# A delta-rule recurrence on one core: nine-block operands, sums moved into the matmul accumulator, four chain banks, and copies moved from VectorE to ScalarE

## The chip, the core and the metric

The kernel runs on one core of a Trainium2 chip. A core has a matrix engine (TensorE: PE for its matmuls, PEld for the loads of its stationary operand), VectorE (DVE), ScalarE (ACT), GpSimd (POOL), and SyncE (SP), which here only issues transfers. All engines work through queues of their own in order and wait for each other by semaphores. Matmuls write to PSUM, eight banks of 128 partitions by 512 f32 values. The metric is the device time of one execution in microseconds (us); lower is better.

## What is computed

The reference is a trunk of four layers: a gated spatial unit, an RWKV-7 layer, a latent attention layer, and a second gated unit. All is f32. The change lies in the RWKV layer alone. Its heart is a recurrence over 256 context tokens and 256 tokens that start from the context's state, for 16 heads of width 64, in two directions; the directions' outputs are added and normalized per head:

```python
def step(S, inp):
    w_t, k_t, v_t, kk_t, a_t = inp[:5]
    s_kk = jnp.einsum('nbhvk,nbhk->nbhv', S, kk_t)
    S = S * w_t[..., None, :] - s_kk[..., :, None] * (kk_t * a_t)[..., None, :] + v_t[..., :, None] * k_t[..., None, :]
    y_t = jnp.einsum('nbhvk,nbhk->nbhv', S, inp[5]) if emit else None
    return S, y_t
...
y = ys[0] + jnp.flip(ys[1], axis=1)
...
mean = jnp.mean(yh, axis=-1, keepdims=True)
var = jnp.mean(jnp.square(yh - mean), axis=-1, keepdims=True)
yn = ((yh - mean) * lax.rsqrt(var + RWKV_LN_EPS)).reshape(y.shape) * ln_gain + ln_bias
```

## The kernel before, in words

The recurrence is done in chunks of 64 tokens: eight chunks (four of the context, four of the sequence), one after the other. The 16 heads are split into four groups g of four heads; with the two directions a group has four "lanes" l (direction n, pair pr), and each lane holds two heads h, one in partitions 0 to 63 and one in 64 to 127 (`H[h]`).

Per group there are these pieces of work:

- `features` makes the operands of four lanes, one lane after another: on GpSimd a `+1` (L659) and the products K (L694), on VectorE a running sum (L667), the products AR (L680, L681), a few more (L685, L688) and the products B (L695). K and B go to the tile BK, eight tiles per group, in the form `[128, 4 chunks, 2, 64]`. For head h, block h of a chunk holds K and block 1-h holds B, so that a chunk's two blocks are one matmul operand of 128 columns.
- `inverse` solves a 64 by 64 triangular system per chunk and head: matmuls `nab` (L717), copies, a transpose, a loop of 31 steps of two VectorE operations each (L734, L735), transposes back (L739, L741) and small matmuls `pg` (L754) and `px` (L765).
- `operands`, per pair of chunks: matmuls `pe` (L785) into the two PSUM banks of tag "s", masked by VectorE into E (L789), loads of UV, and four 128 by 128 transposes of BK per chunk (`pbk`, L805) into the one bank of tag "t", copied by ScalarE to BKT (L806).
- `chain`, per chunk: `pz` (L829, L831), copied by ScalarE to Z (L833); `pu` (L838), whose halves are copied into UV, one by ScalarE (L839) and one by VectorE (L840); `py` from the old state (L845); `pd` (L852), to which VectorE adds the old state (L856) and multiplies by the decay (L857), which gives the new state S; and `py` from UV (L861). `py` holds both directions. The first direction that reaches a place of Y is copied there by ScalarE (L870), and the second is added by VectorE (L872).
- `gate` (matmuls `pg`, L895), `bonus`, `normed` and `added` (matmuls `op`, L966) turn Y into the layer's output. `normed` takes the mean over each head by a matmul with the block matrix `bdm` (`pmean`, L937), subtracts it on VectorE (L938), squares on ScalarE (L941), takes the variance by another matmul (`pvar`, L943) and multiplies (L945).

Tag "c" has three PSUM banks. pz, pu, py, pd, pg, the bonus, the mean, the variance and op of the first three groups all take them in turn. Tags "f" and "n" have one bank each.

`interleave` merges the source of these pieces: while the chain of group g runs, the features and the inverse of group g+1, the gates of g and the output of earlier groups are laid around it. The framework that builds the program then orders each engine's instructions further by their dependencies, so the order on an engine is not strictly that of the source. Values and the features and inverse of group 0 come before the first chain.

## Time before, and the profile

| what | us |
|---|---|
| median of three runs | 1627.66 (1627.23 to 1628.16) |
| the profiled execution | 1626.01 |
| its span, first to last instruction | 1623.8 |
| PE busy | 1521.5 |
| DVE busy | 1173.6 |
| ACT busy | 786.9 |
| POOL busy | 123.3 |

Times in the views are counted from the start of the span. The RWKV recurrence, from the values to the last output, lies between 548 and about 1057 us. An f32 matmul appears as two matmul records (two passes), each with its own weight load; a transpose appears as one. A matmul's record includes the time in which its result runs out of the array, so a record of a back-to-back matmul is longer than its place in the queue: what one costs is read from start to start. The granted clock (PEclk) is the share of TensorE's full 2.4 GHz that it was given; 0.5 is 1.2 GHz.

### The profile page before, as it was taken

Reading aid. Unit: us, or ns where it says so; the run is one execution under the profiler, and the core shown is the slowest. Engines: PE = TensorE matmul, PEld = TensorE weight load, DVE = VectorE, ACT = ScalarE, POOL = GpSimd, SP = SyncE. Lnnn points to the kernel's source line nnn. Section 1 sums busy time; section 2 is a strip of 40 time slices with the busy share of each in tenths; the row PEclk is TensorE's granted clock in tenths of the full one; section 3 lists DMA queues with packets and bytes.
Section 4 is the critical chain, followed back from the end, with each engine's and each line's share of the span. In section 5 each row is a group of like instructions: output and inputs, shape, how many; then the busy total and the mean of one; then the engine's idle time right before and its main releaser. Section 6 shows DMA issues by size and latency. Waiting matters only on the chain.

```text
span 1623.8 us, 28689 instructions
## 1 busy us (share of the span) xinstructions
PE 1521.5 (94%) x11538; PEld 1182.9 (73%) x11538; DVE 1173.6 (72%) x2133; ACT 786.9 (48%) x1404; POOL 123.3 (8%) x156
## 2 busy tenths in 40 slices
PE   5999999999599998999999999889999999979999
PEld 2787888888466644776776777778777777768887
DVE  3789998844878376687877964778765666665876
ACT  4534321232456343435345333469876766456543
POOL 0000000000600232302203100000000000000000
PEclk9999999999799998899999999989999999989999
DMA  9675668531144552522322132144321232265552
GB/s 363 252 281 226 233 212 306 208 104 52 52 143 169 161 164 66 157 92 76 118 91 85 61 106 88 67 144 136 118 83 43 73 99 91 66 233 186 177 182 78
DMA packets 95173, 229.03 MB, mean 141 GB/s; under 512 B 26048, under 2 KB 52160, under 8 KB 80576
## 3 DMA queue, kind: packets, MB, share of 16 engines
q1 hardware_dynamic: 92736, 223.00, 40.6%
q10 hardware_dynamic: 2304, 4.20, 0.7%
q8 instruction: 91, 1.49, 0.4%
q14 instruction: 42, 0.34, 0.1%
HBM read 208.81 MB, written 17.83 MB: 140 GB/s over the span
## 4 chain that ended last, share of the span: by engine, by line
PE 49%; DVE 14%; ACT 3%; issue 2%; POOL 1%; DMA 1%; ACTq 0%; DVEq 0%
PE fm L310 5%; PE op L310 4%; PE op L966 2%; PE fm L311 2%; PE pg L895 2%; DVE Tm L735 2%; DVE tmp L734 2%; PE op L311 2%; PE pu L310 2%; PE pz L310 2%; PE po L1277 2%; PE sc L1295 2%; PE pe L785 2%; PE sc L1296 1%; DVE BK L695 1%
## 5 line engine op out<-in xcount | busy, mean ns | idle before, releaser
L184 DVE TENSOR_TENSOR lo<-raw,hi 128x2048 fp32r<-128x2048 f32 (+3 forms) x147 | 247.1, 1682 | 105.2 <-ACT hi L183 104.5
L183 ACT CAST hi<-raw 128x2048 fp32r<-128x2048 f32 (+3 forms) x161 | 212.3, 1324 | 217.5 <-PE op L314 40.5
L251 DVE SCALAR_TENSOR_TENSOR junk<-adaw,scb 128x1024 f32<-128x1024 f32 x112 | 136.8, 1222 | 8.7 <-DMA adaw<-in_ada_wT 6.7
L310 PE MATMUL op<-s,hi 128*128 128x512 f32 x256 | 91.5, 400 | 0.0
L375 PE MATMUL pv<-hi,hp 128*128 128x512 f32 x192 | 76.4, 400 | 9.1 <-ACT hi L183 6.0
L376 PE MATMUL pv<-lo,hp 128*128 128x512 f32 x192 | 76.2, 397 | 1.7 <-DVE lo L184 1.7
L310 PE MATMUL fm<-hx,hi 128*128 128x512 f32 x200 | 73.8, 409 | 4.1 <-ACT hx L304 3.8
L377 PE MATMUL pv<-hi,hp 128*128 128x512 f32 x192 | 75.9, 395 | 0.0
L311 PE MATMUL op<-s,lo 128*128 128x256 f32 x256 | 71.3, 281 | 0.0
L895 PE MATMUL pg<-xz,wz 128*128 128x256 f32 x256 | 68.7, 408 | 0.0
L313 PE MATMUL pj<-xs,hi 128*128 128x512 f32 x128 | 53.6, 420 | 12.5 <-ACT xs L304 10.2
L311 PE MATMUL fm<-hx,lo 128*128 128x256 f32 x200 | 56.6, 288 | 2.0 <-DVE lo L184 2.0
L995 PE MATMUL pv<-wv,xv 128*128 128x512 f32 x128 | 57.3, 596 | 0.0
L310 PEld LDWEIGHTS op<-s,hi 128*128 128x128 f32 x256 | 48.0, 188 | 12.4 <-issue 1.3
L314 PE MATMUL pj<-xs,hi 128*128 128x512 f32 x128 | 52.2, 408 | 5.0 <-DVE xs L305 5.0
L694 POOL TENSOR_TENSOR BK<-f 64x256 f32<-64x256 f32 x64 | 53.5, 836 | 38.1 <-DVE f L688 30.7
L785 PE MATMUL pe<-AR,BK 64*128 64x128 f32 x512 | 53.8, 306 | 2.2 <-DVE E L789 2.0
L310 PE MATMUL fm<-cq,hi 128*128 128x512 f32 x144 | 55.7, 423 | 0.0
L895 PEld LDWEIGHTS pg<-xz,wz 128*128 128x128 f32 x256 | 47.8, 198 | 10.0 <-issue 2.1
L315 PE MATMUL pj<-xs,lo 128*128 128x512 f32 x128 | 52.1, 408 | 2.2 <-DVE lo L184 2.1
L313 PE MATMUL pu<-hp,hi 128*128 128x512 f32 x128 | 50.7, 396 | 0.0
L789 DVE TENSOR_TENSOR E<-pe,masks 128x512 f32<-128x512 f32 x64 | 41.9, 683 | 12.1 <-PE pe L785 7.2
(392 smaller groups left out, 4063.2 us busy)
## 6 DMA issues: line engine op xcount, KB each, us to landing
adaw<-in_ada_wT SPq DMA_DIRECT2D x36, 1024.0 KB, 6.2
raw<-in_sgu_v SPq DMA_DIRECT2D x16, 1024.0 KB, 5.5
raw<-in_sgu_u SPq DMA_DIRECT2D x16, 1024.0 KB, 4.9
raw<-in_sgu_z SPq DMA_DIRECT2D x16, 1024.0 KB, 4.8
raw<-in_sgu_o SPq DMA_DIRECT2D x16, 1024.0 KB, 4.8
adaw<-in_ada_w SPq DMA_DIRECT2D x24, 512.0 KB, 10.0
xz<-xz SPq DMA_DIRECT2D x32, 256.0 KB, 3.0
raw<-in_ml_z SPq DMA_DIRECT2D x16, 512.0 KB, 3.7
```

What stands on the lines that cost most here:

```text
L183: S.copy(hi[:, sl], raw[:, sl])
L184: (nc.gpsimd if parts > 1 and i else V).tensor_tensor(lo[:, sl], raw[:, sl], hi[:, sl], ALU.subtract)
L251: V.scalar_tensor_tensor(out=junk, in0=raw[:, f, :], scalar=1.0, in1=scb[:, c, :], op0=ALU.mult, op1=ALU.mult, accum_out=m[:, t * 2 + f, c ...
L310: PE.matmul(p, whi, x, start=start, stop=False)
L311: PE.matmul(p[:, 0:256], wlo, x[:, 0], start=False, stop=stop)
L313: PE.matmul(p, whi, x[:, 0], start=start, stop=False)
L375: PE.matmul(pv[tb], hs[k][:, 0, sl], whi[:, ws_], start=k == 0, stop=False)
L376: PE.matmul(pv[tb], hs[k][:, 0, sl], wlo[:, ws_], start=False, stop=False)
L377: PE.matmul(pv[tb], hs[k][:, 1, sl], whi[:, ws_], start=False, stop=k == 7)
L785: PE.matmul(pe[h][:, j * 128:j * 128 + 128], bk[H[h], i % 4, :, :], ar[H[h], i % 4, :, :], start=True, stop=True)
L895: PE.matmul(p, ws[k // 4][:, k % 4, pr * 128:pr * 128 + 128], xs[k // 2][:, k % 2, :], start=k == 0, stop=k == 7)
L995: PE.matmul(p, xv[:, k, tb * 128:tb * 128 + 128], ws[k // 4][:, k % 4, :], start=k == 0, stop=k == 7)
```

## The change

BK becomes `[128, 9 blocks, 64]` per tile. K of head 0 goes to blocks 0, 2, 4, 6, K of head 1 to blocks 2, 4, 6, 8, and B of both heads to blocks 1, 3, 5, 7, so that one VectorE operation over 128 partitions writes B where there were two over 64. A chunk's operand for head h is two neighbouring blocks from block `2*(i % 4) + h`.

The transposes of BK are done per head: 64 partitions by 128 columns, so eight per chunk where there were four. They go into the two banks of tag "s", one bank for each head, both chunks of a pair side by side, and are copied by ScalarE when both chunks are there. Tag "t" is given up, and tag "c" has four banks.

In the chain the second half of `pu` is copied by ScalarE too. `pd` starts with two matmuls of the identity with the old state, 256 columns each, and accumulates onto them; the VectorE addition is gone. The two directions of `py` are copied to two tiles (Y and Yr), all by ScalarE. `normed` multiplies both by `center` (the identity minus `bdm`) into one accumulator, which is the sum of directions less its mean, so the subtraction is gone; the square and the product read the accumulator.

The scratch memory for GpSimd-generated transfers is set to 1024 bytes, which leaves room for the larger tiles.

```diff
+        center = const.tile([128, 128], F32, name="center")
+        V.tensor_tensor(center, ident, bdm, ALU.subtract)
...
-        env["ps"] = (("f", 1), ("n", 1), ("s", 2), ("t", 1), ("c", 3))
+        env["ps"] = (("f", 1), ("n", 1), ("s", 2), ("c", 4))
...
-                        bk = st(f"BK{sg}", [128, 4, 2, 64], 8)
+                        bk = st(f"BK{sg}", [128, 9, 64], 8)
                         for h in range(2):
-                            nc.gpsimd.tensor_tensor(bk[H[h], :, h, :], k4[H[h], sg], c4[H[h], sg], ALU.mult)
-                            V.scalar_tensor_tensor(out=bk[H[h], :, 1 - h, :], in0=b4[H[h], sg], scalar=-0.5, in1=c4[H[h], sg],
-                                                   op0=ALU.mult, op1=ALU.mult)
+                            nc.gpsimd.tensor_tensor(bk[H[h], 2 * h:2 * h + 7:2, :], k4[H[h], sg], c4[H[h], sg], ALU.mult)
+                        V.scalar_tensor_tensor(out=bk[:, 1:8:2, :], in0=b4[:, sg], scalar=-0.5, in1=c4[:, sg], op0=ALU.mult, op1=ALU.mult)
...
+        def stacked(bk, h, i):
+            j = 2 * (i % 4) + h
+            return bk[H[h], j:j + 2, :].rearrange("p a s -> p (a s)")
...
+            pb = [ps("pbk", "s") for h in range(2)]
             for ii in range(2):
-                bt = d["bk", ii] = ct("BKT", [128, 4, 2, 64], 2)
                 i = i2 * 2 + ii
-                pb = ps("pbk", "t")
                 for l in range(4):
-                    PE.transpose(pb[:, l * 128:l * 128 + 128], f["BK"][l, i // 4][:, i % 4, :, :].rearrange("p a b -> p (a b)"), ident)
-                S.copy(bt.rearrange("p l h k -> p (l h k)"), pb)
-                yield
+                    for h in range(2):
+                        PE.transpose(pb[h][:, (ii * 4 + l) * 64:(ii * 4 + l) * 64 + 64], stacked(f["BK"][l, i // 4], h, i), ident[H[h], H[h]])
+                if ii == 0:
+                    yield
+            for h in range(2):
+                d["bk", h] = ct("BKT", [128, 2, 4, 64], 4)
+                S.copy(d["bk", h].rearrange("p i l k -> p (i l k)"), pb[h])
+            yield
...
-                V.tensor_copy(uv[H[0], 1, ii], pu[H[0]])
+                S.copy(uv[H[0], 1, ii], pu[H[0]])
...
-                    pd = q4(ps("pd", "c"))
+                    pd = ps("pd", "c")[:, 0:256]
+                    if s0 is not None:
+                        for h in range(2):
+                            PE.matmul(pd[H[h]], ident[:, H[h]], s0.rearrange("p l v -> p (l v)"), start=True, stop=False, skip_group_check=True)
+                    pd = pd.rearrange("p (l v) -> p l v", l=4)
                     for l, h in LH:
-                        PE.matmul(pd[H[h], l], bk[:, l, h, :], uv[:, h, ii, l], start=True, stop=True)
+                        PE.matmul(pd[H[h], l], bk[h][:, l, :], uv[:, h, ii, l], start=s0 is None and l == 0, stop=l == 3, skip_group_check=True)
                     sn = ct("S", [128, 4, 64], 2)
-                    pcb = f["12"][:, :, i:i + 1].to_broadcast([128, 4, 64])
-                    if s0 is not None:
-                        V.tensor_tensor(sn, pd, s0, ALU.add)
-                        V.tensor_tensor(sn, sn, pcb, ALU.mult)
-                    else:
-                        V.tensor_tensor(sn, pd, pcb, ALU.mult)
+                    V.tensor_tensor(sn, pd, f["12"][:, :, i:i + 1].to_broadcast([128, 4, 64]), ALU.mult)
...
-                for n in range(2):
-                    y = yt[:, :, (3 - c) * 64:(4 - c) * 64][:, :, ::-1] if n else yt[:, :, c * 64:c * 64 + 64]
-                    if c < 2:
-                        S.copy(y, py[:, n * 2:n * 2 + 2])
-                    else:
-                        V.tensor_tensor(y, y, py[:, n * 2:n * 2 + 2], ALU.add)
+                S.copy(yt[0][:, :, c * 64:c * 64 + 64], py[:, 0:2])
+                S.copy(yt[1][:, :, (3 - c) * 64:(4 - c) * 64][:, :, ::-1], py[:, 2:4])
...
-            PE.matmul(pm, bdm, y, start=True, stop=True)
-            V.tensor_tensor(y, y, pm, ALU.subtract)
+            PE.matmul(pm, center, y, start=True, stop=False)
+            PE.matmul(pm, center, cut(f["Y"][c][1]), start=False, stop=True)
             yield
             sq = cut(ct("fin", [128, 2, 256], 3))
-            S.activation(sq, y, AF.Square)
+            S.activation(sq, pm, AF.Square)
             pq = flat(ps("pvar", next(tags)))
             PE.matmul(pq, bdm, sq, start=True, stop=True)
             state["act"] = rsqrt_bc(sq, pq, 1.0, epsln)
-            V.tensor_tensor(y, y, sq, ALU.mult)
+            V.tensor_tensor(y, pm, sq, ALU.mult)
...
-                f["Y"].append(ct("Y", [128, 2, 256], 3))
+                f["Y"].append([ct("Y", [128, 2, 256], 3), ct("Yr", [128, 2, 256], 3)])
...
-    nc = _bacc.Bacc("TRN2", target_bir_lowering=False, num_devices=1)
+    nc = _bacc.Bacc("TRN2", target_bir_lowering=False, num_devices=1, dynamic_dma_scratch_size=1024)
```

Tag "t" in the lists of banks at the end of the layer becomes "c"; the operand of `nab` (L717) is addressed by its block.

## Rows read from the trace of the kernel before

**Rows 1.** The page's first part: busy time of each engine, its share of the span and its instructions.

```profile
PE 1521.5 (94%) x11538; PEld 1182.9 (73%) x11538; DVE 1173.6 (72%) x2133; ACT 786.9 (48%) x1404; POOL 123.3 (8%) x156
```

**Rows 2.** Ten stretches that cover the recurrence: the stretch, its length in us, the busy us and (instructions) of PE, PEld, DVE, ACT and POOL in this order, the granted clock as a share of 2.4 GHz, the transfers' share and GB/s; the last line adds them up. 548 to 664 is the values with group 0's features and inverse; 664 to 700, 760 to 802 and 867 to 911 hold the features of groups 1, 2 and 3; 700 to 760, 802 to 867 and 911 to 970 their inverses; 970 to 1030 the chain of group 3; 1030 to 1057 the last output.

```profile
548.00:630.00 82.00, 79.37 (x448) 36.82 (x446) 62.01 (x131) 37.39 (x69) 24.28 (x27) 1.00 0.49 132
630.00:664.00 34.00, 27.70 (x387) 22.12 (x387) 19.07 (x31) 14.24 (x24) 10.39 (x13) 0.60 0.43 125
664.00:700.00 36.00, 31.73 (x629) 25.68 (x629) 22.59 (x48) 17.36 (x42) 11.34 (x12) 0.95 0.46 141
700.00:760.00 60.00, 57.84 (x924) 44.31 (x920) 51.34 (x126) 25.68 (x50) 7.85 (x10) 1.00 0.27 81
760.00:802.00 42.00, 37.52 (x574) 27.48 (x573) 34.72 (x68) 22.04 (x45) 15.64 (x18) 0.92 0.35 107
802.00:867.00 65.00, 61.38 (x970) 47.79 (x968) 53.18 (x129) 26.03 (x52) 6.62 (x8) 1.00 0.27 88
867.00:911.00 44.00, 39.23 (x583) 28.75 (x584) 35.43 (x67) 22.21 (x45) 17.54 (x21) 0.92 0.29 86
911.00:970.00 59.00, 55.31 (x896) 43.65 (x895) 45.28 (x116) 20.56 (x40) 2.03 (x4) 1.00 0.28 87
970.00:1030.00 60.00, 58.20 (x828) 45.63 (x828) 27.01 (x59) 21.31 (x46) 0.00 (x0) 1.00 0.32 107
1030.00:1057.00 27.00, 22.47 (x193) 17.95 (x189) 21.88 (x65) 13.96 (x36) 0.00 (x0) 0.95 0.07 22
sum 509.00, PE 470.75 PEld 340.19 DVE 372.51 ACT 220.78 POOL 95.70; mean PE 47.08 PEld 34.02 DVE 37.25 ACT 22.08 POOL 9.57
```

**Rows 3.** Who waited for whom between 548 and 1057 us: the waiting engine and line, the instruction waited for, us in total, times, the longest.

```profile
DVE UV L840 <- ACT UV L839: 22.0, 10, 5.8
PE pg L754 <- DVE Dm L739: 8.4, 4, 5.7
PE pd L852 <- DVE UV L840: 6.8, 6, 2.2
PE pz L829 <- DVE z L900: 3.7, 1, 3.7
PE pe L785 <- DVE E L789: 2.0, 4, 0.7
```

**Rows 4.** The timeline of one chunk of group 1's chain: start, duration, engine, line and operation.

```profile
787.22 0.37 ACT L839 COPY UV<-pu 64x256 f32<-64x256 f32 x1
787.80 1.23 DVE L667 TENSOR_TENSOR_SCAN f<-cmask,f 128x512 f32<-128x512 bf16 x1 [0.68 <-POOL BK L694]
792.25 0.41 DVE L840 COPY UV<-pu 64x256 f32<-64x256 f32 x1
793.33 0.69 PE L852 MATMUL pd<-UV,BKT 128*64 128x64 f32 x16
```

**Rows 5.** Groups of instructions of one line and shape between 548 and 1057 us: count, busy us, mean ns of one, idle time before them.

```profile
L695 DVE SCALAR_TENSOR_TENSOR BK<-f 64x256 f32<-64x256 f32 x64 | 39.5, 617 | 1.5 <-ACT f L670 0.5
L840 DVE COPY UV<-pu 64x256 f32<-64x256 f32 x32 | 13.1, 410 | 22.0 <-ACT UV L839 22.0
L856 DVE TENSOR_TENSOR S<-pd,S 128x256 f32<-128x256 f32 x24 | 10.0, 418 | 4.9 <-PE pd L852 4.8
L872 DVE TENSOR_TENSOR Y<-Y,py 128x128 f32<-128x128 f32 x32 | 8.5, 282 | 0.0
L938 DVE TENSOR_TENSOR Y<-Y,pmean 128x512 f32<-128x512 f32 x7 | 4.8, 684 | 4.0 <-PE pmean L937 4.0
L839 ACT COPY UV<-pu 64x256 f32<-64x256 f32 x32 | 11.7, 367 | 32.9 <-PE pu L838 29.3 <-DMA xz<-xz 3.2
L870 ACT COPY Y<-py 128x128 f32<-128x128 f32 x32 | 7.0, 271 | 11.0 <-PE py L861 11.0
```

**Rows 6.** Line L695 alone: count, least, median and greatest duration in ns.

```profile
L695 DVE SCALAR_TENSOR_TENSOR BK<-f x64: 405/460/972, 562.1 to 903.5; 64x256 f32<-64x256 f32 x64
```

**Rows 7.** TensorE's timeline in a stretch without waits, with the shape of the tile (rows*columns) and of the streamed operand; xN is the number of passes. From the start of a row to the start of the next is what its passes cost.

```profile
970.87 1.16 PE L785 MATMUL pe<-AR,BK 64*128 64x128 f32 x16
971.96 1.99 PE L895 MATMUL pg<-xz,wz 128*128 128x256 f32 x8
973.89 0.69 PE L852 MATMUL pd<-UV,BKT 128*64 128x64 f32 x16
974.40 0.64 PE L861 MATMUL py<-E,UV 128*64 128x64 f32 x16
974.97 1.12 PE L937 MATMUL pmean<-Y,bdm 128*128 128x512 f32 x2
975.93 0.60 PE L805 MATMUL pbk<-ident,BK 128*128 128x128 f32 x4
976.37 1.89 PE L895 MATMUL pg<-xz,wz 128*128 128x256 f32 x8
978.19 0.34 PE L829 MATMUL pz<-UV,E 64*64 64x64 f32 x4
```

**Rows 8.** TensorE's timeline around its longest wait of the recurrence.

```profile
629.53 0.48 PE L643 MATMUL pw<-wx,w2w 128*128 128x512 f32 x1
635.75 1.92 PE L754 MATMUL pg<-Dm,X 32*32 32x32 f32 x64 [5.74 <-DVE Dm L739]
```

More of the change, by code (lines that the diff above doesn't have):

```diff
@@ L717, in inverse @@
                             PE.matmul(pn[64 * h + 32 * hf:64 * h + 32 * hf + 32, i * 64:i * 64 + 64 - 32 * hf],
-                                      bk[H[h], i % 4, 1 - h, 32 * hf:32 * hf + 32], ar[H[h], i % 4, 0, 32 * hf:64], start=True, stop=True)
+                                      bk[H[h], 2 * (i % 4) + 1, 32 * hf:32 * hf + 32], ar[H[h], i % 4, 0, 32 * hf:64], start=True, stop=True)
                 p8 = pn.rearrange("p (i t) -> p i t", i=8)
@@ L784, in operands @@
                             bk, ar = f["BK"][l, i // 4], f["AR"][l, i // 4]
-                            PE.matmul(pe[h][:, j * 128:j * 128 + 128], bk[H[h], i % 4, :, :], ar[H[h], i % 4, :, :], start=True, stop=True)
+                            PE.matmul(pe[h][:, j * 128:j * 128 + 128], stacked(bk, h, i), ar[H[h], i % 4, :, :], start=True, stop=True)
                 for h in range(2):
@@ L824, in chain @@
                 e = lambda l, h: d["E", l % 2, h][:, ii, l // 2]
-                uv, bk = d["uv"], d["bk", ii]
+                uv, bk = d["uv"], [d["bk", h][:, ii] for h in range(2)]
                 q4 = lambda p: p[:, 0:256].rearrange("p (l v) -> p l v", l=4)
@@ L934, in normed @@
             tags = iter("fn" if g == 3 else "cc")
-            y, z, b = cut(f["Y"][c]), cut(f["z"][c]), cut(b)
+            y, z, b = cut(f["Y"][c][0]), cut(f["z"][c]), cut(b)
             pm = flat(ps("pmean", next(tags)))
-            PE.matmul(pm, bdm, y, start=True, stop=True)
-            V.tensor_tensor(y, y, pm, ALU.subtract)
+            PE.matmul(pm, center, y, start=True, stop=False)
+            PE.matmul(pm, center, cut(f["Y"][c][1]), start=False, stop=True)
             yield
             sq = cut(ct("fin", [128, 2, 256], 3))
-            S.activation(sq, y, AF.Square)
+            S.activation(sq, pm, AF.Square)
             pq = flat(ps("pvar", next(tags)))
@@ L959, in added @@
             cut, flat = quarters(q)
-            y = cut(f["Y"][c])
+            y = cut(f["Y"][c][0])
             for oo in range(4):
@@ L1050, in rwkv @@
         ws = [wout(3, oo, t.rearrange("p a (b c) -> p a b c", b=2)) for oo, t in enumerate((wz[0][:, 2:4], wz[1][:, 0:2], wz[1][:, 2:4], ct("z", [128, 2, 256], 3)))]
-        op30 = added(3, f, 0, "csct", ws=ws)
+        op30 = added(3, f, 0, "cscc", ws=ws)
         interleave((islice(steps, 12), 12), (chained(late, normed(3, f, 0), bonus(3, 1, b)), 11))
         interleave((steps, 4), (normed(3, f, 1, b, slice(1, 3)), 4), (islice(op30, 1), 2))
-        interleave((normed(3, f, 1, b, slice(0, 4, 3)), 3), (chained(op30, added(3, f, 1, "sstc", slice(1, 3), ws)), 7))
-        interleave(added(3, f, 1, "sftn", slice(0, 4, 3), ws))
+        interleave((normed(3, f, 1, b, slice(0, 4, 3)), 3), (chained(op30, added(3, f, 1, "sscc", slice(1, 3), ws)), 7))
+        interleave(added(3, f, 1, "sfcn", slice(0, 4, 3), ws))
         cstack.close()
```

## The prediction

> **What bounds the kernel now.** I read the page's first part, then the recurrence by stretches, then who waits for whom, then TensorE's order of work. The page puts TensorE at 94% of the span and VectorE at 72% [rows 1]. The change touches only 548 to 1057 us. There TensorE is busy 470.75 of 509 us [rows 2], so at most 38.25 us are waits. The last stretch's 4.53 belong to the hand-over to the next layer, which leaves 33.7.
>
> The second loss is the clock. Its shortfall times the stretch's length is 0.40 x 34 = 13.6 us at 630, 0.05 x 36 = 1.8 at 664, 0.08 x 42 = 3.4 at 760 and 0.08 x 44 = 3.5 at 867, together 22.3 us [rows 2]. The reader is to see where they lie: in the features of each group and just after a long wait. The engine stands still for 5.74 us before 635.75 because VectorE's transpose Dm is late [rows 8], and the stretch from 630 to 664 has a granted clock of 0.60, a mix of 1.2 and 2.4 GHz.
>
> So TensorE is the bound and VectorE is what makes it wait. The waits named after VectorE are Dm 8.4, UV 6.8, z 3.7 and E 2.0, 20.9 of the 33.7 [rows 3]. One chunk shows how. ScalarE's half of UV starts at 787.22 and is done at 787.6, but VectorE's half starts only at 792.25, behind a running sum and other feature work, and pd starts at 793.33 [rows 4]. In the inverses VectorE is busy 51.34 of 60 and 53.18 of 65 us; in group 3, which has no features ahead, 27.01 of 60, and TensorE's waits fall to 1.8 us [rows 2].
>
> **What leaves VectorE.** B: 64 operations become 32 of twice the partitions. Each new one costs between 0.405 and 0.972 us [rows 6]; I take the mean of 0.617 [rows 5], since GpSimd still writes the same tiles beside it. That saves 32 x 0.617 = 19.7. The copies of UV go: 13.1. The old state's addition: 10.0. The directions' addition: 8.5. The mean's subtraction: 4.8 for the seven whole ones and about 0.8 for two halves (estimate, half of 0.684 with overhead) [rows 5]. Together 56.9 of VectorE's 372.51 us, 15%. The one new operation, center, is 128 by 128 and made once, 0.28 us by the addition of that size [rows 5], ahead of the recurrence.
>
> **What comes to ScalarE.** 32 copies at 0.367 and 32 at 0.271 us, 20.4 us on 220.8 [rows 2, 5]: 47% of 509. The copies of BKT keep their elements. Behind each added copy the next copy of Z may wait. Were all on the path, that is 20.4 us; TensorE's work of the other pieces covers them, as it does for most waits in the inverses, and I take nothing. Against that, UV's second half no longer passes a semaphore and a foreign queue: in the chunk shown it would start at 787.6 in place of 792.25 [rows 4]. If pd starts that much earlier, what is late next is E, which VectorE masks behind the same feature work (2.0 us today [rows 3]).
>
> **What comes to TensorE.** First, the identity matmuls: two per chunk with an old state, 24 chunks, two passes each, 256 columns. A pass of 256 columns costs (978.19 - 976.37) / 8 = 0.228 us on the whole array. A pass of pd, which has the same tile of 128*64, costs 0.51 / 16 = 0.032 for 64 columns, where a quarter of 0.228 would be 0.057: the two column halves overlap [rows 7]. Four passes cost 0.91 without overlap and 0.51 with all of it, 24 chunks 12.2 to 21.8 us. I take 0.6, since the row of the same tile overlaps and only the last pass has no partner: +14.4. They need the old state alone, so they can run while UV is copied; their cover is the very wait that the change removes.
>
> Second, the mean: a second matmul of two passes, 0.96 us [rows 7], seven times, and two of half the columns at 0.48 (estimate, half): +7.7, on the in-order queue with nothing that hides it.
>
> Third, the transposes: 128 passes at 0.44 / 4 = 0.11 us, 14.1 us, become 256 of 64 rows and 64 streamed columns. The nearest row is pe, same tile of 64*128, 128 columns: 1.09 / 16 = 0.068 [rows 7]. Half of that, 0.034, is the lower bound (-5.4 us), and a pass as dear as today's the upper (+14.1). I take 0.04, nearer to pe since it is the same tile: -3.9.
>
> On this third term the Trainium skill speaks against the change. The row: pe loads 128 columns for each pass and still takes 0.068 us a pass [rows 7]. "TensorE: Matmul & The Clock Gate", section "LDWEIGHTS (loading the stationary operand)", says that a load's time goes by the columns alone, columns / 1.2 in ns, whatever the rows: 107 ns for 128 columns, so 256 loads would cost 27.4 us (an estimate from that page), +13.3 in place of -3.9, and the sum below would be 17 us higher. The rows of pe do not bear it out where row halves alternate.
>
> TensorE in all: +18.2 us, between +14.5 and +43.6.
>
> **Banks.** Tag "c" gains a bank. The wait for one, pz behind z, is 3.7 us in all [rows 3], and most of that can go; but the mean's accumulator is now held until the last product, so a normalization takes two banks at once. The transposes move to tag "s", behind E's two masks. Today's waits of pe for these masks are 2.0 us [rows 3]; as many again for the transposes would be 2. I net these to -1, inside the next term.
>
> **What the waits give back.** UV's 6.8 go. Of Dm's 8.4 I take half: it lies behind a loop of VectorE whose own operations stay, and only the feature work mixed into it shrinks. Of z's 3.7 and E's 2.0 I take 4 with the net above, and 2 of the 12.8 unnamed: 17 of 33.7, between 6.8 (UV alone) and 33.7. Of the clock's 22.3 I take half, 11.2: most of the 8.7 after 664, whose waits are UV's, and about a third of the 13.6 at 630, where 5.74 us would shrink to about 3. Its bounds are 0 and 22.3. No transfer is moved or added; the smaller scratch serves transfers that GpSimd makes, and the code issues none there.
>
> **The sum.** The profiled execution took 1626.0 us (span 1623.8 and 2.2 around it). 1626.0 + 18.2 - 17 - 11.2 = 1616.0. The median of the runs shown is 1.65 above that execution, so I forecast 1617.7. A measurement of this kernel tells about 0.2%, 3.3 us, from no change.
>
> **Rivals.**
> - *The added passes cost nothing.* If TensorE's records hide room, the 18.2 us fit between the other passes: 1599.5. For it: loads are busy only 340.19 of 509 us, 67% [rows 2]. Against it: start to start, the passes of 970 to 978 leave no room [rows 7]. The Trainium skill, "Perfetto Trace Analysis", section "Identifying the Most-Contended Engine", holds matmul busy time a bad measure and the loads' busy share a better one; by that rule the engine has a third to spare. The trace agrees with it only where there are waits. Chance 0.19; the same time comes out if the low clock goes altogether and a bit more of the waits.
> - *The low clock stays.* Waits of 2 to 3 us remain ahead of each feature stretch, as at 630, and the 11.2 are not given back: 1628.9, no change. For it: half of Dm's waits stay by my own count. Chance 0.14.
> - *TensorE only has more to do.* The side that ends slower: VectorE's freed time becomes idle time, since in-order work of other pieces (the loop of the inverse, E) sets TensorE's waits. Only UV's 6.8 go and the clock does not: 1627.7 + 18.2 - 6.8 = 1639. For it: TensorE is at 97% in group 3's chain [rows 2], where little can be gained and six chunks grow. It decides as soon as less than 18.2 of the 56 us come back. Chance 0.15.
> - *The transposes are bound by their loads.* 256 passes at today's 0.11 us: 18 us over the forecast, 1635.7. For it: each pass still loads 128 columns. Against it: pe. Chance 0.09.
>
> **How the numbers follow.** The forecast has 0.43; its own range, from a quarter more or less of the 28.2 us given back, is 1610.7 to 1624.7. Faster is the forecast and the first rival, 0.62; same 0.14; slower 0.24. The range goes from 1599, about the first rival's time, which leaves half of its 0.19 below, to 1638, which leaves some 0.1 of the slow cases above.
>
> **What would show it.** Right: L840, L856, L872 and L938's subtraction gone and VectorE near 316 us in 548 to 1057; the wait of pd for UV near nothing; identity passes at about 0.6 us a chunk; transposes at about 0.04 us a pass; no wait over 4 us before pg L754 and a granted clock above 0.60 behind it. Wrong: waits of the same sum under other names (E, s banks, Z), a clock as low as now, or transposes at 0.07 us and more.

## The result and the profile after

| what | before | after |
|---|---|---|
| median, us | 1627.45 | 1637.5 (1636.83 to 1641.57) |
| the profiled execution | 1626.01 | 1636.83 |
| its span | 1623.8 | 1635.0 |

The changed kernel is 0.6% slower: ratio 1.006, 95% interval 1.0043 to 1.0077. The forecast was 1617.7. Line numbers are higher by 2 to 14 than before. One later execution, 2476 us at a granted clock of 0.556, belongs to a slow state and is in no figure below.

The page's first part after the change, to read beside [rows 1]:

```profile
PE 1530.6 (94%) x11780; PEld 1184.3 (72%) x11780; DVE 1127.2 (69%) x2005; ACT 805.2 (49%) x1468; POOL 124.4 (8%) x156
```

VectorE lost 46 us, TensorE gained 9, and the span grew by 11. Stretches of the changed kernel, to read beside [rows 2] (the last line adds up ten stretches from 548 to 1070):

```profile
630.00:664.00 34.00, 27.25 (x485) 21.90 (x487) 16.45 (x29) 15.92 (x29) 6.83 (x10) 0.75 0.56 164
664.00:700.00 36.00, 31.32 (x589) 24.42 (x585) 22.19 (x42) 16.91 (x43) 12.01 (x13) 0.95 0.34 104
...
760.00:802.00 42.00, 38.07 (x588) 27.18 (x589) 27.85 (x55) 23.36 (x50) 16.43 (x18) 0.96 0.39 116
802.00:867.00 65.00, 61.89 (x990) 47.12 (x980) 46.67 (x109) 28.35 (x59) 6.18 (x8) 0.97 0.26 79
867.00:911.00 44.00, 41.29 (x649) 30.00 (x648) 28.11 (x54) 24.39 (x54) 18.02 (x21) 0.96 0.30 92
911.00:970.00 59.00, 53.32 (x877) 40.84 (x876) 39.53 (x95) 22.81 (x49) 2.03 (x4) 0.94 0.25 78
970.00:1030.00 60.00, 58.85 (x753) 45.95 (x753) 18.74 (x37) 20.45 (x48) 0.00 (x0) 1.00 0.31 99
1030.00:1070.00 40.00, 33.11 (x382) 25.78 (x380) 25.44 (x68) 22.34 (x58) 0.00 (x0) 0.99 0.13 45
sum 522.00, PE 478.71 PEld 341.26 DVE 326.55 ACT 239.65 POOL 96.84; mean PE 47.87 PEld 34.13 DVE 32.65 ACT 23.96 POOL 9.68
```

The stretches are 13 us longer in all. TensorE stands still for 522 - 478.7 = 43.3 us; less the 6.9 of the last stretch that is 36.4, where it was 33.7. So VectorE became idler and TensorE waits no less. Who TensorE waits for now, to read beside [rows 3]:

```profile
PE pg L756 <- DVE Dm L741: 10.6, 4, 5.3
PE pd L868 <- ACT UV L851: 7.5, 5, 1.8
PE pe L792 <- DVE E L796: 3.3, 1, 3.3
PE nab L719 <- ACT X L724: 2.9, 3, 1.3
PE pu L849 <- ACT Z L844: 2.3, 3, 1.0
```

The wait of pd for UV has only changed its name, from VectorE to ScalarE's second copy (6.8 to 7.5 us). The wait of pz for z is gone (3.7), but nab and pu wait for ScalarE (2.9 and 2.3, with 1.1 and 1.4 before), and Dm's wait is no shorter.

What the added passes cost, on TensorE's timeline of the changed kernel, to read beside [rows 7] (start to next start):

```profile
970.81 1.02 PE L812 MATMUL pbk<-ident,BK 64*128 64x64 f32 x16
971.76 0.70 PE L973 MATMUL op<-Y,wo 128*128 128x256 f32 x2
...
981.59 1.13 PE L944 MATMUL pmean<-Y,center 128*128 128x512 f32 x2
982.55 1.02 PE L945 MATMUL pmean<-Yr,center 128*128 128x512 f32 x2
983.41 1.89 PE L902 MATMUL pg<-xz,wz 128*128 128x256 f32 x8
...
991.10 0.65 PE L865 MATMUL pd<-S,ident 128*64 128x256 f32 x4
991.58 0.98 PE L868 MATMUL pd<-UV,BKT 128*64 128x64 f32 x15
...
994.08 0.71 PE L812 MATMUL pbk<-ident,BK 64*128 64x64 f32 x8
994.71 0.70 PE L902 MATMUL pg<-xz,wz 128*128 128x256 f32 x2
```

The second mean matmul takes 0.86 us, the identity passes of a chunk 0.48, a transpose 0.95 / 16 = 0.059 to 0.63 / 8 = 0.079. Added up over the recurrence from start to start, with waits cut out, the identity takes 12.6 us, the mean 14.1 in place of 7.2, and the transposes 16.7 in place of 17.1: 19.1 us in all.

Where the time is lost can be read from the writing of the new state S. First before, then after, the sixth chunk of group 2 and the last state of group 3:

```profile
938.89 0.41 DVE L857 TENSOR_TENSOR S<-S,12_5976 128x256 f32<-128x256 f32 x1
...
1030.50 0.42 DVE L857 TENSOR_TENSOR S<-S,12_7356 128x256 f32<-128x256 f32 x1
```

```profile
937.24 0.42 DVE L870 TENSOR_TENSOR S<-pd,12_6011 128x256 f32<-128x256 f32 x1
...
1041.41 0.42 DVE L870 TENSOR_TENSOR S<-pd,12_7423 128x256 f32<-128x256 f32 x1 [0.81 <-PE pd L868]
```

At the first of them the changed kernel is still 1.6 us ahead; at the second it is 10.9 behind. The whole loss falls into these last 104 us (92 before), where hardly any feature work is left and TensorE is busy for 99.1 us (88.9 of 92 before).

### The profile page after: what moved, and what is told of

Read it like the earlier page. It is cut to its first block, busy times and chain, and to the rows that moved or that the text cites. A ratio compares the mean times of both kernels' runs of the same rounds, so it can differ in the third digit from the quotient of the medians.

```text
span 1635.0 us, 29065 instructions
## 1 busy us (share of the span) xinstructions
PE 1530.6 (94%) x11780; PEld 1184.3 (72%) x11780; DVE 1127.2 (69%) x2005; ACT 805.2 (49%) x1468; POOL 124.4 (8%) x156
## 3 DMA queue, kind: packets, MB, share of 16 engines
q1 hardware_dynamic: 92736, 223.00, 40.5%
## 4 chain that ended last, share of the span: by engine, by line
PE 45%; DVE 9%; ACT 5%; issue 1%; POOL 1%; DMA 0%; SPq 0%; ACTq 0%; DVEq 0%; POOLq 0%
PE fm L310 4%; PE op L310 4%; PE pg L902 2%; PE op L973 2%; PE fm L311 2%; PE op L311 2%; PE pz L310 2%; PE pu L310 2%; PE po L1284 2%; DVE Tm L737 2%; DVE tmp L736 2%; PE sc L1302 2%; PE pe L792 1%; PE sc L1303 1%; PE pv L376 1%
## 5 line engine op out<-in xcount | busy, mean ns | idle before, releaser
L183 ACT CAST hi<-raw 128x2048 fp32r<-128x2048 f32 (+3 forms) x161 | 212.3, 1324 | 217.6 <-PE op L314 40.5
L902 PE MATMUL pg<-xz,wz 128*128 128x256 f32 x256 | 72.7, 424 | 0.0
L313 PE MATMUL pj<-xs,hi 128*128 128x512 f32 x128 | 53.5, 420 | 12.6 <-ACT xs L304 10.2
L310 PEld LDWEIGHTS op<-s,hi 128*128 128x128 f32 x256 | 48.1, 188 | 12.5 <-issue 1.3
L977 DVE SCALAR_TENSOR_TENSOR xT<-op,mod,xT 128x256 f32<-128x256 f32 (+1 forms) x72 | 29.9, 447 | 38.5 <-PE op L973 38.4
L973 PE MATMUL op<-Y,wo 128*128 128x256 f32 x192 | 53.2, 408 | 0.0
```

The costliest lines, as they stand in the source:

```text
L183: S.copy(hi[:, sl], raw[:, sl])
L310: PE.matmul(p, whi, x, start=start, stop=False)
L902: PE.matmul(p, ws[k // 4][:, k % 4, pr * 128:pr * 128 + 128], xs[k // 2][:, k % 2, :], start=k == 0, stop=k == 7)
L973: PE.matmul(p[:, ob], w[:, k, ob, :], y[:, k], start=k == 0, stop=k == 1)
```

## How the experiments are read

Three parts of the change can be undone one by one: **U**, UV's second half on ScalarE; **I**, the identity matmuls for the old state; **M**, the directions' sum and the mean in the accumulator, with two tiles of Y copied by ScalarE. What is left without them is the base: nine blocks, transposes by halves, four chain banks, smaller scratch.

The executions of one kernel differ by up to 17 us here, and go with their mean granted clock: an execution with 0.01 less is some 8 us longer. A fit over 262 executions of nineteen kernels (one time for each kernel, one common slope) gives 8.4 us for each 0.01 and leaves 1.7 us unexplained. Each kernel is therefore given by its median and by its time at a granted clock of 0.97, from that fit ("at 0.97"). The kernel before: 1627.0 at 0.97; the changed one: 1637.8. The fit shows that time and clock go together, not which of them sets the other. Where a part itself lowers the clock, the time at 0.97 leaves that share of its cost out; so the medians stand beside it.

| parts | median, us | ratio to before, 95% | at 0.97 |
|---|---|---|---|
| base | 1617.5 | 0.993 (0.9906 to 0.9954) | 1619.5 |
| base, three chain banks | 1630.5 | 1.0018 (1.0000 to 1.0035) | 1626.6 |
| U | 1627.6 | 0.9985 (0.9966 to 1.0004) | 1624.0 |
| I | 1626.3 | 0.9995 (0.9981 to 1.0008) | 1627.7 |
| M | 1638.3 | 1.0056 (1.0037 to 1.0074) | 1630.1 |
| U, I | 1623.7 | 0.9978 (0.9960 to 0.9996) | 1625.3 |
| U, M | 1635.5 | 1.0045 (1.0028 to 1.0063) | 1630.6 |
| I, M | 1635.9 | 1.0042 (1.0023 to 1.0061) | 1635.1 |
| U, I, M: the change | 1637.5 | 1.0060 (1.0043 to 1.0077) | 1637.8 |

## Which part costs

P is the theory that TensorE's passes set the time and each costs its place; W, that the loss lies in waits that moved.

**Without I** (U and M stay): VectorE adds the old state again.

```diff
-                        for h in range(2):
-                            PE.matmul(pd[H[h]], ident[:, H[h]], s0.rearrange("p l v -> p (l v)"), start=True, stop=False, skip_group_check=True)
+                        V.tensor_tensor(sn, pd, s0, ALU.add)
+                        V.tensor_tensor(sn, sn, pcb, ALU.mult)
```

> The changed kernel with the old state added by VectorE again, without the two identity matmuls. Theory P (TensorE is the bound, and each added pass costs its full place in its queue): the 96 identity passes held the queue for 12.6 us, so 1637.5 - 12.6 = 1625, with some 2 us of the VectorE addition's wait given back: 1624 to 1628. Theory W (the loss lies in waits that moved, ahead of pg L756 and nab L719): it gives back less than half of that, 1632 to 1638.

**Without M** (U and I stay): one Y, and the mean as before.

```diff
-                S.copy(yt[0][:, :, c * 64:c * 64 + 64], py[:, 0:2])
-                S.copy(yt[1][:, :, (3 - c) * 64:(4 - c) * 64][:, :, ::-1], py[:, 2:4])
+                    if c < 2:
+                        S.copy(y, py[:, n * 2:n * 2 + 2])
+                    else:
+                        V.tensor_tensor(y, y, py[:, n * 2:n * 2 + 2], ALU.add)
...
-            PE.matmul(pm, center, y, start=True, stop=False)
-            PE.matmul(pm, center, cut(f["Y"][c][1]), start=False, stop=True)
+            PE.matmul(pm, bdm, y, start=True, stop=True)
+            V.tensor_tensor(y, y, pm, ALU.subtract)
```

> The changed kernel with one tile Y, the second direction added by VectorE, the mean by bdm and the subtraction by VectorE, as in the kernel before. Theory P: the second mean matmul held TensorE's queue for 6.9 us (14.1 in place of 7.2), so 1637.5 - 6.9 = 1630.6, 1629 to 1633. Theory W: no change, 1635 to 1639, since VectorE gets 14 us back and is late again.

**Without both** (U stays):

> The changed kernel with both undone: what stays is the nine-block operands with their transposes, the four chain banks and the copies of UV on ScalarE. Theory P: 1637.5 - 19.5 = 1618, 1616 to 1622, which is under the kernel before, because VectorE keeps 33 us of its relief. Theory W: 1630 to 1638.

**Without U** (I and M stay):

```diff
-                S.copy(uv[H[0], 1, ii], pu[H[0]])
+                V.tensor_copy(uv[H[0], 1, ii], pu[H[0]])
```

> The changed kernel with the second half of UV copied by VectorE again. Theory P: the copies are on no bound engine, within 3 us of 1637.5. Theory W, in its form that ScalarE is now late (nab waits 5.9 us for copies L724 that waited 0 to 4 before): faster by 4 us and more, 1630 to 1634. Should the copy on ScalarE be what removes the 6.8 us of waits of pd for UV, then slower by up to 7, 1644.

Measured in this order: 1635.5, 1623.7, 1627.6, 1635.9. The first lies in the range of W, the last in that of P, the two between in neither. M alone of the three moves the median far: without it the kernel is 13.8 us faster and ahead of the one before, which neither theory had expected. At 0.97 M costs 12.5 us there and I 7.2, for 6.9 and 12.6 us of passes.

The same parts added to the base, **M** and **I** by themselves:

> The kernel with only the nine blocks, the transposes by halves and the four banks (1617.5 us) plus the accumulator's sum and mean, that is two tiles of Y copied by ScalarE and two matmuls with center; UV's second half on VectorE and the old state added by VectorE as before. Each part has its own price whatever stands beside it: the sum and mean cost 12 to 14 us, 1629 to 1633. The price hangs on what the other parts put on ScalarE and TensorE: its bare 7 us of passes less some relief of VectorE, 1620 to 1625.

> The same kernel (1617.5 us) plus the identity matmuls alone; UV's second half on VectorE, sum and mean as before. Each pass costs its place: 1628 to 1632. The passes fill the wait of pd for UV, which is there with VectorE's copy too (10 us of waits before pd): 1616 to 1622. The same with a VectorE relief that pays: below 1615.

They took 1638.3 and 1626.3 us, both outside every range expected. M costs 21 us by the medians and 10.6 at 0.97; I 9 and 8.2. Over the four pairs of the table at 0.97, M costs 6.6 to 12.5 (mean 9.3), I 1.3 to 8.2 (mean 5.4), U -2.4 to 4.5 (mean 1.3). So M costs more than its passes, I less than half of its own, and U, which takes 13.1 us from VectorE [rows 5], brings nothing. The price of one part swings by 6 to 7 us with what stands beside it, so a single pair of kernels does not give it closely.

## What VectorE's relief is worth

**VectorE's work put back.** B is written twice, and the new state is summed twice into eight columns that nobody reads. Whatever reads BK waits for the second writing of B, so this part is not pure load, and the cost is an upper bound for load.

```diff
                         V.scalar_tensor_tensor(out=bk[:, 1:8:2, :], in0=b4[:, sg], scalar=-0.5, in1=c4[:, sg], op0=ALU.mult, op1=ALU.mult)
+                        V.scalar_tensor_tensor(out=bk[:, 1:8:2, :], in0=b4[:, sg], scalar=-0.5, in1=c4[:, sg], op0=ALU.mult, op1=ALU.mult)
...
+                    V.tensor_reduce(out=dummy[:, 0:4], in_=sn, op=ALU.add, axis=AX.X)
+                    V.tensor_reduce(out=dummy[:, 4:8], in_=sn, op=ALU.add, axis=AX.X)
```

> The changed kernel with VectorE work put back that nothing waits for: B is written twice (32 more operations of some 0.6 us) and the new state is summed twice into eight unused columns (56 more of some 0.4 us), about 42 us of the 46 that VectorE lost between 548 and 1057. Theory U (what VectorE was relieved of was idle time already, TensorE's own order and passes set the time): within 3 us of the changed kernel, 1634 to 1641. Theory V (the relief did pay, 17 to 28 us as in the prediction, and the passes cost that much more than their places): 1648 to 1665.

Its added groups of instructions:

```profile
L700 DVE SCALAR_TENSOR_TENSOR BK<-f 128x256 f32<-128x256 f32 x32 | 17.4, 558 | 0.1
...
L873 DVE TENSOR_REDUCE dummy<-S 128x4 f32<-128x256 f32 x28 | 11.6, 415 | 0.3
L874 DVE TENSOR_REDUCE dummy<-S 128x4 f32<-128x256 f32 x28 | 11.5, 411 | 0.0
```

17.4 + 11.6 + 11.5 = 40.5 us of VectorE cost 8.6 us by the median (1646.1), and 3.8 at 0.97: between the two theories and far nearer to the one by which the relief was idle time. A tenth of VectorE's time comes back, and with what goes with the clock (a mean of 0.964 against 0.9695) a fifth. TensorE's two largest waits do not grow with the load (10.6 and 7.5 us in the changed kernel):

```profile
PE pg L758 <- DVE Dm L743: 10.2, 4, 5.3
PE pd L870 <- ACT UV L853: 7.8, 5, 1.8
```

**The base alone** (VectorE 23 us lighter by the page, no streamed columns added):

> The kernel before with only the nine blocks, the transposes by halves, the four banks and the smaller scratch; both halves of UV, the old state, the directions and the mean as before. VectorE loses 19.7 us, TensorE's transposes cost the same by the traces (17.1 and 16.7 us). If VectorE's relief is worth nothing: 1624 to 1629. If it is worth a quarter to a half of itself: 1617 to 1623. If the two banks of the masks are the trouble: 1630 to 1636.

**The base with three chain banks:**

```diff
-        env["ps"] = (("f", 1), ("n", 1), ("s", 2), ("c", 4))
+        env["ps"] = (("f", 1), ("n", 1), ("s", 2), ("c", 3))
```

> The same kernel (1617.5 us) with three chain banks in place of four; the bank that held the transposes before stays empty. The 10 us came from the fourth bank: 1624 to 1630. They came from VectorE's 19.7 us less for B and the pair-wise transposes: 1616 to 1620.

The base is the fastest kernel of the study, 1617.5 us, 0.7% ahead of the one before. By itself that lies in the range for a relief that pays. But with three banks it falls to 1630.5, so the gain is the fourth bank's (13 us by the medians, 7.1 at 0.97) and not B's: with three banks the lighter VectorE gives 0.4 us at 0.97. The first lines of the pages of the base and of the base with three banks:

```profile
PE 1510.2 (94%) x11666; PEld 1169.7 (73%) x11666; DVE 1150.1 (71%) x2101; ACT 787.6 (49%) x1404; POOL 125.3 (8%) x156
```

```profile
PE 1523.1 (94%) x11666; PEld 1180.4 (73%) x11666; DVE 1153.1 (71%) x2101; ACT 787.4 (48%) x1404; POOL 123.9 (8%) x156
```

The same 11666 passes take 13 us less of TensorE's busy time with four banks; a part of that is the clock, 0.976 against 0.968 in these two executions. TensorE's waits between 548 and 1070 us are no shorter with the fourth bank (40.8 us against 39.2); what differs is the time from pass to pass, in part with the clock there (0.97 against 0.95 from 548 to 1030). How the bank shortens that was not found.

## What an added pass is worth

**The mean's matmul twice** (on the kernel without M; the second issue overwrites the first):

```diff
             PE.matmul(pm, bdm, y, start=True, stop=True)
+            PE.matmul(pm, bdm, y, start=True, stop=True)
```

> The changed kernel with the directions' sum and the mean done as before (one Y, the second direction added by VectorE, the mean subtracted; 1623.7 us so far), but with the matmul of the mean issued twice, the second over the first, so that the two extra passes per normalization come alone (7 x 0.96 and 2 x 0.48 us by the start-to-start prices, 7.7 us). Three theories for the 13.8 us that the accumulator's sum and mean cost. Passes (they cost twice their place, because they stand where the chain has nothing else to run): 1634 to 1639. Bank (the mean's accumulator is kept until the product, so that the chain turns in three banks): the passes alone cost their place, 1628 to 1632. Copies (ScalarE's two copies per chunk more, and a Y that is complete later): 1624 to 1632.

**A bank held, without a pass** (on the same kernel; the subtraction is gone, and the square reads `pm` as well):

```diff
-            PE.matmul(pm, bdm, y, start=True, stop=True)
-            V.tensor_tensor(y, y, pm, ALU.subtract)
+            PE.matmul(pm, center, y, start=True, stop=True)
...
-            V.tensor_tensor(y, y, sq, ALU.mult)
+            V.tensor_tensor(y, pm, sq, ALU.mult)
```

> As the kernel with the sum and the mean done as before, but the mean's one matmul takes center in place of bdm on the summed Y; no subtraction, and the square and the product read the accumulator, which is so kept until the product. No extra pass, no extra copy, a bank held longer. Passes: 1620 to 1624 (VectorE loses its subtraction). Bank: 1629 to 1636. Copies: 1620 to 1624.

**ScalarE's copies, without pass and bank** (on the changed kernel):

```diff
-            PE.matmul(pm, center, y, start=True, stop=False)
-            PE.matmul(pm, center, cut(f["Y"][c][1]), start=False, stop=True)
+            V.tensor_tensor(y, y, cut(f["Y"][c][1]), ALU.add)
+            PE.matmul(pm, bdm, y, start=True, stop=True)
+            V.tensor_tensor(y, y, pm, ALU.subtract)
```

> The changed kernel with the two tiles of Y, all copied by ScalarE as in the change, which VectorE then adds once per normalization; the mean is a single matmul with bdm and is subtracted as before. ScalarE's copies alone, without extra passes and without the long-held bank. Passes and bank: 1621 to 1627. Copies: 1633 to 1639.

**The bank freed early** (on the changed kernel, the square and the product from Y):

```diff
+            V.tensor_copy(y, pm)
```

> The changed kernel with one VectorE copy of the mean's accumulator into Y as soon as it is done, and the square and the product from there: extra passes and ScalarE's copies stay, the bank comes free early. Passes and copies: 1636 to 1641. Bank: 1627 to 1632.

Medians 1636.4, 1633.8, 1627.7, 1636.1; at 0.97 1636.1, 1631.7, 1628.2, 1637.5. Against 1625.3 without M, the second matmul alone costs 10.8 us, the held bank alone 6.4, the copies alone 2.9; M as a whole costs 12.5, so these do not add. Each of the first two medians lies in the range of its own theory (passes, bank), the copies' just above the range that gives them nothing, and the bank freed early in that for passes. By these pairs passes alone suffice for nearly all of it, and freeing the bank beside them gives nothing back.

**The normalization in the banks of tags f and n**, in the changed kernel and in the base:

```diff
-            tags = iter("fn" if g == 3 else "cc")
+            tags = iter("fn")
```

> The changed kernel with the mean's and the variance's accumulators of the first three groups in the banks of tags f and n, which the features and the inverses use, so that the chain has its four banks to itself. If the sum and mean cost more than their 7 us of passes because they take chain banks (the fourth is worth 7 us at the same granted clock): 1628 to 1633. If the passes alone count: 1635 to 1640. If they now stop the features and inverses: 1641 to 1650.

> The kernel with only the nine blocks, the transposes by halves and four banks (1617.5 us, the fastest so far), with the mean's and the variance's accumulators in the banks of tags f and n. If chain banks are still short with four: 1611 to 1616. If not: 1616 to 1621. If the features and inverses are stopped: 1622 to 1630.

1650.5 and 1629.7 (1646.6 and 1626.2 at 0.97): slower by 9 and 7 us at the same clock, so features and inverses are held up more than the chain is freed. These two runs do not tell whether the chain is still short of banks.

**The identity twice**, on the kernel without M, and **the whole identity in one matmul**:

```diff
                         for h in range(2):
                             PE.matmul(pd[H[h]], ident[:, H[h]], s0.rearrange("p l v -> p (l v)"), start=True, stop=False, skip_group_check=True)
+                        for h in range(2):
+                            PE.matmul(pd[H[h]], ident[:, H[h]], s0.rearrange("p l v -> p (l v)"), start=True, stop=False, skip_group_check=True)
```

> The kernel with the sum and the mean done as before (1623.7 us) with the two identity matmuls of the old state issued twice, the second over the first: 24 x 0.53 = 12.6 us of passes more, at the place where pd waits for UV (3.8 us of waits there with the identity once, 8 to 10 without it). If passes there fill a wait first: the first issue has filled most of it, so this second one costs nearly its place, 1632 to 1637. If they cost nothing at all there: 1622 to 1626. If an added pass costs one and a half times its place as the second mean matmul did (7.0 us of passes, 12.6 us of time): 1640 to 1645.

```diff
-                        for h in range(2):
-                            PE.matmul(pd[H[h]], ident[:, H[h]], s0.rearrange("p l v -> p (l v)"), start=True, stop=False, skip_group_check=True)
+                        PE.matmul(pd, ident, s0.rearrange("p l v -> p (l v)"), start=True, stop=False, skip_group_check=True)
```

> The kernel with the sum and the mean done as before, and the old state brought in by one matmul with the whole identity (two passes of 256 columns, 0.456 us by the start-to-start price) in place of two on half the columns (0.53): 1.8 us of TensorE less. TensorE's passes set the time: 1620 to 1624, at or below that kernel. Waits for UV take the place: no difference.

The second identity costs 15.7 us at 0.97 (median 1639.8, just under the highest of the three ranges) for 11.1 us of passes by its trace (12.6 were expected), where the first cost 1.3 (U against U, I). Waits before pd fall from 6.7 us (U alone) to 3.4 with the first identity and stay at 3.5 with the second; all of TensorE's waits up to the last state go from 38.1 to 30.9 and 30.7. So the first filled some 7 us of waits and the second none; the rest of the difference is not explained by waits. In the base, where the same waits fall from 8.7 to 4.4, the first costs 8.2. The one matmul, which should have saved 1.8 us, came out 2.4 us slower at 0.97 (median 1629.9), above both ranges. Each edit also changes the order in which the framework lays out the instructions; a difference of 2 to 3 us between two of these kernels is therefore not read as the edit's own, and how large such effects can grow was not tested.

## Why the forecast failed, step by step

**What bounds the kernel**: right. TensorE is the bound; added passes that found no wait to fill cost their place and more (second identity 15.7 for 11.1, second mean matmul 10.8 for 7.0).

**TensorE's 18.2 us**: right in sum, 19.1 by the trace, and that by luck: its three errors, -1.8, -0.8 and +3.5, nearly cancel. The identity is 12.6 where 14.4 was taken (0.525 a chunk for 0.6), the mean's second matmul 6.9 for 7.7. The transposes were mis-sized: 0.059 to 0.079 us a pass in place of 0.04, so the 3.9 us of gain are 0.4; those of before took 17.1, not 14.1. Loads do not bind them: 256 passes in 16.7 us are 0.065 each. The Trainium skill's rule for loads by columns ("TensorE: Matmul & The Clock Gate", "LDWEIGHTS (loading the stationary operand)") would make them 107 ns each; the trace does not agree where row halves alternate.

**VectorE's relief of 56.9 us**: near. Durations added up, VectorE lost 54 us of the recurrence; neighbouring records overlap, so its busy time fell by 46, from 372.5 to 326.6, where 316 was the sign named. B gave more than was taken, 39.5 us down to 14.9:

```profile
L698 DVE SCALAR_TENSOR_TENSOR BK<-f 128x256 f32<-128x256 f32 x32 | 14.9, 488 | 1.7 <-ACT f L672 1.4
```

**The 17 us that the waits were to give back**: the step that failed. TensorE's waits went from 33.7 to 36.4 us. The step took VectorE's name behind a wait as a sign that VectorE's load causes it, of UV's 6.8 us in full and of Dm's 8.4 by half. Dm's four waits, first before (with the 5.74 us of [rows 8]) and then after:

```profile
732.19 0.69 PE L852 MATMUL pd<-UV,BKT 128*64 128x64 f32 x16
...
738.80 1.20 PE L754 MATMUL pg<-Dm,X 32*32 32x32 f32 x64 [0.52 <-DVE Dm L739]
...
841.64 1.20 PE L754 MATMUL pg<-Dm,X 32*32 32x32 f32 x64 [1.12 <-DVE Dm L739]
...
949.75 1.20 PE L754 MATMUL pg<-Dm,X 32*32 32x32 f32 x64 [1.01 <-DVE Dm L739]
```

```profile
633.88 1.92 PE L756 MATMUL pg<-Dm,X 32*32 32x32 f32 x64 [5.29 <-DVE Dm L741]
...
731.94 0.65 PE L865 MATMUL pd<-S,ident 128*64 128x256 f32 x2
735.37 1.20 PE L756 MATMUL pg<-Dm,X 32*32 32x32 f32 x64 [2.79 <-DVE Dm L741]
736.50 0.43 PE L865 MATMUL pd<-S,ident 128*64 128x256 f32 x1
...
838.89 1.20 PE L756 MATMUL pg<-Dm,X 32*32 32x32 f32 x64 [1.27 <-DVE Dm L741]
...
947.08 1.20 PE L756 MATMUL pg<-Dm,X 32*32 32x32 f32 x64 [1.24 <-DVE Dm L741]
```

Dm is ready 1.9 to 3.4 us earlier in all four, so the lighter queue did help the inverse. But TensorE reaches pg earlier too, and the waits add up to 10.6 us in place of 8.4. A wait is the distance between two arrivals, and the step moved only one of them. All of the growth is the wait of group 1's inverse, 0.52 to 2.79: before, pd of group 0's seventh chunk ran ahead of that pg (732.19), and now pg stands in the middle of pd's identity passes (731.94 and 736.50). ScalarE had finished UV at 729.5, so the chain, too, stood behind the wait.

The longest wait had little feature work to lose. In 600 to 633.9 us of the changed kernel, ahead of it, VectorE does this:

```profile
L736 DVE TENSOR_TENSOR tmp<-Dm,Tm 128x31 f32<-128x31 f32 (+15 forms) x31 | 11.8, 380 | 0.9
L737 DVE TENSOR_TENSOR Tm<-Tm,tmp 128x31 f32<-128x31 f32 (+15 forms) x31 | 11.7, 377 | 0.9
...
L698 DVE SCALAR_TENSOR_TENSOR BK<-f 128x256 f32<-128x256 f32 x2 | 0.8, 405 | 0.0
```

62 dependent operations take 23.5 of 33.9 us, and B is 0.8 of the rest.

In the chain UV's wait moved to ScalarE. The 0 us taken for ScalarE's added copies left out what else stands in ScalarE's queue:

```profile
717.16 0.37 ACT L850 COPY UV<-pu 64x256 f32<-64x256 f32 x1
717.55 1.28 ACT L279 ACT_TABLE_LOAD   x1
718.84 0.63 ACT L279 ACTIVATE fin<-fin 128x512 f32<-128x512 f32 x1
719.50 0.37 ACT L851 COPY UV<-pu 64x256 f32<-64x256 f32 x1
...
719.91 0.62 PE L868 MATMUL pd<-UV,BKT 128*64 128x64 f32 x13 [1.41 <-ACT UV L851]
```

Between the two copies the normalization loads an activation table and runs its Exp, and the second copy starts 2.3 us after the first. This happens in five of the 32 chunks, and these are the five waits of pd, 7.5 us in all. The chunk of [rows 4] went much as forecast, 5.03 us between the copies down to 1.04, with only one feature operation of ScalarE between them:

```profile
790.25 0.37 ACT L850 COPY UV<-pu 64x256 f32<-64x256 f32 x1
790.64 0.63 ACT L672 ACTIVATE f<-f 128x512 f32<-128x512 f32 x1
791.29 0.37 ACT L851 COPY UV<-pu 64x256 f32<-64x256 f32 x1
```

Without U the kernel is 1.6 us faster, no more than the order of the instructions may make.

**The clock's 11.2 us**: hardly any of it came. The shortfall of the stretches up to 1030 is 19.2 us in the profile (22.3 before), 8.5 of it at 630, where the clock is 0.75 for 0.60; but over all executions the mean granted clock is 0.9695 after and 0.9687 before. The step was probably wrong in its weight, too: it counted a shortfall as time lost in full, which is 16.3 us for 0.01 of 1630, and in the executions 8.4 us go with it.

**Banks, netted to -1**: mis-sized. The fourth bank is worth 7.1 us at 0.97 where it was measured, in the base: the largest gain found.

With the sizes measured, the sum is 1626.0 + 19.1 - 7.1 + 1.65 = 1639.7, with nothing for waits and clock; measured were 1637.5. That it comes so near is in part luck: taken out one by one, I costs less than its passes and M more. Nearest is the rival "TensorE only has more to do", forecast at 1639, whose condition, that less than 18.2 of the 56 us come back, was met. Its reason holds as well: the loss lies where group 3's chain runs, with TensorE at 95% and more. Its number owes something to luck, for the 6.8 us that it took from UV's wait did not come, and the bank's 7.1, which it did not have, did. Of the loss of 12.5 us in those last stretches the added passes are 6.7 (identity 3.7, mean 1.9, transposes 1.1); more and dearer passes of pg and op, at a clock of 0.97 for 1.00, are another 5.5. "The low clock stays" had the clock right, but the waits that it still counted on did not shrink. "The transposes are bound by their loads", 1635.7, is near in time, but not by its condition, 0.11 us a pass. "The added passes cost nothing" fell with the second mean matmul. The rule of the Trainium skill behind it ("Perfetto Trace Analysis", "Identifying the Most-Contended Engine") reads the loads' busy share, 72% here, as the better measure; by the runs that share was no room for passes outside of waits.

**Open** are three things: why M's passes cost more than their place, why a held bank costs 6.4 us without them and nothing beside them, and what the fourth bank shortens.

## What to carry to other kernels

Before work is moved from an idle engine's queue onto the bound engine, ask what sets both ends of the wait that it is to shorten: when the awaited result is ready, and when the bound engine gets to it. Here the first moved by 2 to 3 us and the wait grew. Before an operation is moved to another queue, look at what stands in that queue at its place, in every chunk and not in one. In these runs a pass added to the bound engine was paid in full, or more, unless it ran inside a wait that stayed, and a wait that one pass had filled hid nothing of the next. When a change bundles parts, time the parts apart: here the base without U, I and M is 20 us faster than the whole.

## What was not expected of the hardware

- Of the granted clock's shortfall about half shows beside the time: 8.4 us for 0.01 where the whole would be 16.3 of 1630 us. Executions of one kernel on one chip lay between 0.959 and 0.975, and 1642.1 and 1625.6 us (the held-bank kernel).
- B's VectorE operation is as long over 128 partitions as over 64; the long ones are among those with GpSimd at work beside them. Of the 64 operations before, the 13 without a GpSimd operation beside them take 413 ns in the mean and the other 51 take 669; of the 32 after, the 8 without take 420 and the 24 others 511. So the 204 ns by which the mean of 617 [rows 5] lies above 413 came with GpSimd. The median went from 460 [rows 6] to 418:

```profile
L698 DVE SCALAR_TENSOR_TENSOR BK<-f x32: 404/418/951, 561.1 to 902.3; 128x256 f32<-128x256 f32 x32
```

- Each of the five reciprocal roots that ScalarE takes for the normalization between 700 and 940 us loads an activation table twice, 1.28 us each time: ahead of the logarithm and ahead of the Exp. UV's first copy was laid right behind the logarithm and its second behind the Exp, which is why the second started 2.3 us after the first.
